# The values of a dilated attention layer: one product of 512 columns per group and four heads, in place of 256 + 256 columns of two groups for two heads

## Chip, cores and metric

One core of one Trainium2 chip runs the kernel in one launch. The metric is the device time of a run in microseconds (us); three runs of the kernel before took 2038.84 to 2041.54, median 2041.24.

## The reference, cut to what matters

Two blocks follow each other: a hybrid attention layer with a mixture of experts, and then a second block with two layers, of which "layer A" is the first. All is float32, 512 tokens of width 1024. Layer A projects the normed tokens to queries, keys and values for three dilation groups of eight heads of width 128, lets each group attend within its own dilated window, and adds the three results with weights from their log-denominators; four further heads read a memory of 256 tokens.

```
DIL_PAIRS = ((128, 1), (512, 4), (2048, 16))          # (window, dilation) of groups 0, 1, 2
qkv = cols.reshape(B, S, 3, N_GROUPS_2, A_HEADS, HEAD_DIM)
q = rms_norm(qkv[:, :, 0], q_gain[:, None, :])
k = rms_norm(qkv[:, :, 1], k_gain[:, None, :])
v = qkv[:, :, 2]                                        # no norm, no rotation
...
for g, (window, dil) in enumerate(DIL_PAIRS):
    o, lse = dilated_window_attention(q[:, :, g], k[:, :, g], v[:, :, g], dil, window // dil)
alpha = jax.nn.softmax(jnp.stack(lses, axis=0), axis=0)
o = jnp.sum(alpha[..., None] * jnp.stack(outs, axis=0), axis=0)
```

## The kernel before, in words

**Products.** A float32 product is made of three matmuls of float32r parts: each operand is split into a high and a low part, and mm3 (L359 to L361) adds high x high, high x low and low x high. The normed, transposed tokens stand in hT, eight pairs of [128 rows of the width, 512 tokens]. A product "natural" takes 128 tokens of hT as the stationary operand (weights of the array, loaded by LDWEIGHTS) and 512 columns of the weight matrix as the moving operand, eight row blocks one after another into one PSUM bank: 24 matmuls, called a pass below; four passes make the 512 tokens.

**Two orders of the tokens.** Tile c holds either the tokens 128 c to 128 c + 127 (run, a plain slice of hT) or the tokens 4 a + c (comb, every fourth element of hT, a slice with a stride of four). Group 0 of the queries, keys and values uses run, groups 1 and 2 use comb. In the text a matmul whose stationary operand is such a slice is called plain or combed.

**Values before.** Per pair of heads, v01_block (L1615) fills one PSUM bank per tile with two products of 256 columns: group 0, plain, in columns 0 to 255, and group 1, combed, in columns 256 to 511. The two halves have different norm factors, so two instructions of 256 columns (L1627) bring them to an SBUF tile of 512. For every second pair, v_block (L1605) makes group 2 for four heads, combed, 512 columns, brought out by one instruction (L1610). The tiles have the tag v, ten places.

**The loop of layer A.** It runs over four pairs of heads (L1762 on). A pair has, in the order of the program: its values (v01_block; in pairs 0 and 2 also v_block of group 2), three qk_block (queries and keys of one group for both heads: a natural product of 512 columns, a norm per head, rotation, four transposes, written to the tag qk of twelve places, all used by a pair), two gate blocks (L1638), and attend_A for each of the two heads. attend_A makes four tiles of scores (L1673, L1676), a softmax on VectorE and ScalarE, transposes (L1681) and the products with the values: groups 1 and 2 of tile c as soon as tile c is there (L1685, L1686), group 0 of all tiles at the end of the head (L1691). So a value tile of groups 1 and 2 comes free within the pair's second head, one of group 0 at its end. After the loop mem_attend handles the memory's heads; its split_kv puts eight tiles into v, its queries eight into qk.

**Order of the work.** The Tile framework's scheduler orders each engine's instructions: by the order of the program, but an instruction may go ahead of earlier ones that wait, as long as its tiles have places. The products of the next pair thus go between the matmuls of a pair's attention. Product sums use the tag acc of two PSUM banks, scores the tag sc of three (at the start of layer A the values use three of sc and one of acc). Weights come in one stream in the order of use: units of 512 KB (two row blocks of 512 columns) are loaded by SyncE's queue into three places wraw, split by ScalarE (L241) and VectorE or, every eighth one, GpSimd (L244), into five places w, each used by 24 matmuls of 512 columns.

Of the kernel before, what the change touches and what calls it, by code (L numbers as in the profile page):

```python
# [11 lines left out]
F32 = mybir.dt.float32  # L12
# [14 lines left out]
NS = 96          # slots of a tile of tokens of one group of experts  # L27


# ---------------------------------------------------------------- host layout  # L30
def _units_k(w, kk):
    """[K, N] -> [K/(128 kk), 128, kk, N]: row blocks, one contiguous run per partition."""
    K, N = w.shape
    return np.ascontiguousarray(w.reshape(K // (128 * kk), kk, 128, N).transpose(0, 2, 1, 3))


def _units_n(w):
    """[K, N] -> [N/128, 128, K/128, 128]: column blocks of 128."""
    K, N = w.shape
    return np.ascontiguousarray(w.reshape(K // 128, 128, N // 128, 128).transpose(2, 1, 0, 3))  # L40


def _cols(v):
    """[128 n] -> [128, n]"""
    return np.ascontiguousarray(v.reshape(-1, 128).T)
# [8 lines left out]
def _nat(t):  # L54
    """[512, n] -> [128, 4, n]"""
    return np.ascontiguousarray(t.reshape(4, 128, -1).transpose(1, 0, 2))


def _constants():
# [22 lines left out]
    # layer A: query 4 a + c in row a of tile c; in group 0 it sees two tiles of 128 keys from BASE[a // 32] on  # L82
# [20 lines left out]
def layout(I):  # L103
# [58 lines left out]
    for hq in range(2):  # L162
        hs0, hs1 = slice(4 * hq, 4 * hq + 2), slice(4 * hq + 2, 4 * hq + 4)
        r = lambda g, hs: v[:, g, hs].reshape(1024, 256)
        vv.append(_units_k(np.concatenate([r(0, hs0), r(1, hs0)], 1), 2))
        vv.append(_units_k(np.concatenate([r(2, hs0), r(2, hs1)], 1), 2))
        vv.append(_units_k(np.concatenate([r(0, hs1), r(1, hs1)], 1), 2))
# [31 lines left out]
# columns of `vecs`  # L199
# [5 lines left out]
class Stream:  # L205
    """Weights in the order of their use: loaded ahead, split into float32r high and low parts."""
# [5 lines left out]
    def lane(self, name, pool, raw, raws, part, parts, pool_every=0, raw_pool=None):  # L212
        """units of this lane are loaded into one of `raws` tiles of tag `raw` and split into one of `parts` pairs"""
        self.lanes[name] = (raw_pool or pool, raw, raws, part, parts, pool_every, pool)
# [32 lines left out]
    def _room(self, first, i, k):  # L247
        """whether there is a place of unit i's tag that none of the units from `first` on takes"""
# [24 lines left out]
    def rows(self, n):  # L273
        """n units of row blocks -> list of (hi, lo) per 128 rows"""
# [7 lines left out]
# steps of the memory's keys and values between the parts of the router, and between the tiles after the experts  # L282
ROUTER = (1, 1, 1, 2, 4, 4, 8)
AFTER = (8, 4, 4, 4, 2, 2)
# products of the next head's q and k, or of the gate, after each level of layer B's scores
FILL = (4, 4, 4, 3, 3, 3, 3)
# steps beside the two attentions of block 1: index scores and products beside the first (its two halves), products
# beside the second
# [3 lines left out]
# when the masks of the best keys are made, in groups of four steps of the first attention  # L292
BEST = {3: 9, 2: 12, 1: 15}
# lanes of the experts' weights: of the first units, then in turns up to units 60, 181 and the end
# [4 lines left out]
def build(tc, A, out, dbg=None):  # L299
# [5 lines left out]
    # ------------------------------------------------------------ pools  # L305
# [23 lines left out]
    # ------------------------------------------------------------ constants  # L329
# [13 lines left out]
    def rsq(pool, ss, n, name="rs", eps=None, ring=""):  # L343
        """(ss / n + eps) ** -0.5 for a [128, m] tile of sums of squares; eps: EPS, or [128, m] or [128, 1]"""
# [12 lines left out]
    def mm3(p, a, b, start, stop):  # L357
        """p += a.T @ b with a, b split into float32r parts; the product of the low parts is below float32."""
# [4 lines left out]
    def split(pool, src, tag, bufs, scale=None):  # L363
        """[128, n] -> float32r high and low parts (of src * scale)."""
# [11 lines left out]
    def row_scale(pool, xs, n=1024):  # L376
        """per-row sums of squares of four natural tiles -> (mean + eps) ** -0.5, [128, len]"""
# [6 lines left out]
    def transposed(xs, gain, pool, tag, bufs, nk=8, banks=(), tps=None, more=None):  # L384
        """natural tiles [128 tok, 128 nk] -> nk pairs (hi, lo) of [128, 128 len(xs)], times a gain per row"""
# [18 lines left out]
    def eps_of(r, name):  # L404
        """EPS / r ** 2: the EPS of a norm of what r has yet to scale"""
# [5 lines left out]
    def norm_tiles(pool, r, combed):  # L411
        """nrm: R the norms r of the rows of four token tiles, RC of the rows 4 a + c, RB along the columns; E, EC: EPS / r ** 2"""
# [15 lines left out]
    def run(c):  # L428
        """token tile c: 128 tokens in a row"""
        return slice(c * 128, c * 128 + 128)  # L430

    def comb(c):
        """token tile c: tokens 4 a + c"""
        return slice(c, None, 4)

    def memory_steps(ws, mT, consume, banks):
        """out[m, 512] = memory @ W for its two tiles of 128, both sums open; consume(c, psum); in steps of one product"""
# [13 lines left out]
    def natural_wide(ws, hT, N, consume, banks):  # L451
        """natural with the four token tiles' sums open"""
# [8 lines left out]
    def natural_steps(ws, hT, N, consume, nunits=4, toks=run, banks=None):  # L461
        """out[tok, N] = h @ W for the four token tiles; consume(c, psum); in steps of one product"""
# [16 lines left out]
    def columns_steps(ws, hT, n, consume, nk=8):  # L479
        """out[128 cols, tok] per column block; consume(j, psum); in steps of one product"""  # L480
# [21 lines left out]
    def pump(steps, n=None):  # L502
        """the next n of the steps, or all that are left"""
# [8 lines left out]
    # ------------------------------------------------------------ streams  # L512
# [21 lines left out]
    for hp in range(4):  # L534
        hq, odd = divmod(hp, 2)
        if odd == 0:
            plan2 += rows_plan(va[3 * hq]) + rows_plan(va[3 * hq + 1])
        else:
            plan2 += rows_plan(va[3 * hq + 2])
# [26 lines left out]
    # ------------------------------------------------------------ shared pieces  # L566
    last = {}

    def softmax_tile(pool, pieces, W, tag):
        """pieces: [(psum ap, mask ap, column)] of negated scores -> normalised weights [128, W]"""  # L570
# [12 lines left out]
    def swap_rope(pool, dst, src, tab, nh, half, eng, tag):  # L583
        """dst, src: [128, nh, 2 half] views; tab: [128, 2, 2 half] = (cos|cos, -sin|sin)"""
# [8 lines left out]
    def outproj(yT, xs, view, after=None):  # L593
        """xs += y @ W, 512 columns at a time with the four token tiles' sums open"""
# [18 lines left out]
    # keys and values of the memory (both layers of the second block)  # L613
    mTd = dr.tile([128, 2048], F32, name="mTd")

    def mem_load(pool):
        """what mem_prep stored, split"""
# [10 lines left out]
    def mem_prep(pool):  # L628
        """the memory's rows normalised, transposed, split for the first layer: 8 pairs of [128 d, 256 m]; stored for
        the second"""  # L630
# [39 lines left out]
    def mem_v(mT, out, banks=(acc, acc)):  # L670
        """values of the memory, in steps of one product: out(c) [128 m, 512] of its tokens 128 c + .."""
        return memory_steps(ws, mT, lambda c, p: S.activation(out(c), p, AF.Copy), banks)

    def mem_k(l, mT, pool, out, banks=(acc, acc)):
        """keys of the memory, in steps of one product and a last one of transposes: out(j) [128 d, 512 (h, m)] of heads 2 j and 2 j + 1"""
# [14 lines left out]
    def head_norm(pool, p, nh, tag, bufs, eps=None, ring=""):  # L690
        """psum [128, 128 nh] -> rows of each head over their root mean square"""
# [10 lines left out]
    # ============================================================ block 1  # L702
# [37 lines left out]
    # c_q, k_r, w_i  # L740
# [40 lines left out]
    def rope_heads(c, p, nh, scale, tag, bufs, dup=False):  # L781
        """natural [128, 64 nh] psum -> scaled, the first 16 of each 64 rotated"""
# [36 lines left out]
    def roped_steps(scale, nat):  # L819
        """the eight heads of 64, natural, in steps of one product"""  # L820
# [9 lines left out]
    # index scores, the 128 best keys of each query  # L830
# [23 lines left out]
    def best(i):  # L854
        """the mask that leaves the 128 best keys of a query"""
# [16 lines left out]
    # MLA, four heads at a time  # L872
# [7 lines left out]
    def attention_steps(prs, lhs, rhs, masks, vt, otag, obufs, res, ahead=2):  # L880
        """pairs of heads of 64: softmax over the keys up to each query tile -> o^T split; in steps of a tile's
        scores, its transposes, or a head's values"""
# [57 lines left out]
    def half_steps(hh):  # L940
        """queries and keys of four heads, in steps of one product"""
# [31 lines left out]
    # DSA  # L973
# [11 lines left out]
    # y = sigmoid(g_a) y_a + sigmoid(g_b) y_b, transposed (the heads' outputs carry the factor 1/2 of the sigmoid)  # L985
    yac, sgb = [], []

    def part_a():
        """in steps of one product"""
# [50 lines left out]
    # ============================================================ router and experts  # L1040
# [86 lines left out]
    # logits of x1 with the gain in the weights; the norm of the row is applied to them  # L1127
# [50 lines left out]
    def first_max(src, n, name):  # L1178
        """src [128, 4, n] -> (max [128, 4], one-hot of its first place [128, 4, n])"""
# [38 lines left out]
    def steps(src, n, name):  # L1218
        """number of whole NS in src"""
# [17 lines left out]
    # weights of the two best experts of the group  # L1237
# [26 lines left out]
    # what a slot has to know of its token: tile + 1, row, 1 / rms (payi); the four weights (payw);  # L1264
    # the last two in three bfloat16 parts
# [20 lines left out]
    def slot_ranks(shift, name):  # L1286
        """[128 tok, NS slots] per token tile: whether the token is of rank shift + slot in its group"""
# [9 lines left out]
    def slot_table(R, pay, n, name):  # L1297
        """[NS slots, 8 groups, n]: what the slot's token of each group wrote"""
# [7 lines left out]
    def slot_rows(t, n, name):  # L1306
        """t [NS, n, 5] -> rows to read and to write (int32 [NS, n]; an empty slot reads row 0 and writes
        row 512 + slot), 1 / rms [NS, n]"""
# [12 lines left out]
    def slot_weights(t, n, name):  # L1321
        """t [NS, n, 12] -> half weights [NS, n, 4]"""
# [31 lines left out]
    def experts(get, X, w, ox):  # L1354
        """the four experts of one group on NS slots: rows of sum_e w_e (silu(x Wg) * (x Wu)) Wd"""
# [60 lines left out]
    # groups with more than NS tokens: at most five further tiles of NS slots  # L1416
# [49 lines left out]
    # x + m, its norm, the input of the second block  # L1466
# [545 lines left out]
```

## Time and profile before

| | us |
|---|---|
| runs | 2041.54, 2038.84, 2041.24; median 2041.24 |
| profiled execution, first to last instruction | 2042.5 |
| PE (TensorE matmul) busy | 1971.9, 97% of the span |
| PEld (weight loads) busy | 1571.2, 77% |
| DVE (VectorE) busy | 1144.4, 56% |
| ACT (ScalarE) busy | 945.9, 46% |
| POOL (GpSimd) busy | 577.0, 28% |

No time outside the span is recorded for the profiled execution; the span itself lies 1.3 us above the median of the runs. Matmuls are pipelined: one's recorded duration overlaps the next one's start, so what a matmul costs in a stream is read from the distance between starts, and idle time of PE from waits. A few matmul records are missing, and a row that says x2 holds two matmuls. Layer A lies between about 898 and 1600 us of the span.

### The profile page before, as it was taken

Reading aid. Unit: us, or ns where it says so; the run is one execution under the profiler, and the core shown is the slowest. Engines: PE = TensorE matmul, PEld = TensorE weight load, DVE = VectorE, ACT = ScalarE, POOL = GpSimd, SP = SyncE. Lnnn points to the kernel's source line nnn. Section 1 sums busy time; section 2 is a strip of 40 time slices with the busy share of each in tenths; the row PEclk is TensorE's granted clock in tenths of the full one; section 3 lists DMA queues with packets and bytes.
Section 4 is the critical chain, followed back from the end, with each engine's and each line's share of the span. In section 5 each row is a group of like instructions: output and inputs, shape, how many; then the busy total and the mean of one; then the engine's idle time right before and its main releaser. Section 6 shows DMA issues by size and latency. Waiting matters only on the chain.

```text
span 2042.5 us, 27315 instructions
## 1 busy us (share of the span) xinstructions
PE 1971.9 (97%) x10138; PEld 1571.2 (77%) x10138; DVE 1144.4 (56%) x1999; ACT 945.9 (46%) x1975; POOL 577.0 (28%) x518
## 2 busy tenths in 40 slices
PE   8999999999899898799999999999999999999999
PEld 8757766787566565589988989888988877777887
DVE  5378744376989986754332341342347344666672
ACT  5454444344667665653443443443456233333460
POOL 2201200011677664631521410530520001222210
PEclk9999999999999998999999999999999999999999
DMA  5211222178788887743211222221223333221231
GB/s 169 78 52 42 62 62 62 52 243 292 262 295 290 328 307 284 248 168 137 83 62 42 83 63 74 84 70 42 83 63 124 103 114 93 63 63 56 70 104 62
DMA packets 77711, 257.08 MB, mean 126 GB/s; under 512 B 10241, under 2 KB 12033, under 8 KB 77569
## 3 DMA queue, kind: packets, MB, share of 16 engines
q1 hardware_dynamic: 74912, 246.33, 36.1%
q0 software_dynamic: 1792, 6.29, 0.9%
q10 hardware_dynamic: 864, 2.62, 0.3%
q8 instruction: 82, 1.34, 0.3%
q14 instruction: 61, 0.49, 0.1%
HBM read 241.58 MB, written 13.63 MB: 125 GB/s over the span
## 4 chain that ended last, share of the span: by engine, by line
PE 54%; DVE 1%; ACT 1%; POOL 0%; issue 0%; DMA 0%; ACTq 0%; DVEq 0%; POOLq 0%
PE acc L359 13%; PE acc L360 13%; PE acc L361 13%; PE sc L359 2%; PE sc L361 2%; PE sc L360 2%; PE sc L1882 1%; PE sc L1673 1%; PE tp L1599 1%; PE sc L1676 1%; PE tp L1681 1%; PE oT L1691 1%; PE oT L1930 1%; ACT whi L241 0%; DVE wlo L244 0%; PE oT L1685 0%
## 5 line engine op out<-in xcount | busy, mean ns | idle before, releaser
L244 DVE TENSOR_TENSOR wlo<-wraw,whi 128x1024 fp32r<-128x1024 f32 (+4 forms) x255 | 335.3, 1321 | 227.9 <-ACT whi L241 226.4
L241 ACT ACTIVATE whi<-wraw 128x1024 fp32r<-128x1024 f32 (+4 forms) x294 | 296.4, 1011 | 296.1 <-PE acc L360 113.7
L359 PE MATMUL acc<-whi,hh 128*128 128x512 f32 (+3 forms) x1040 | 411.0, 397 | 5.2 <-ACT hjk L695 2.6
L360 PE MATMUL acc<-wlo,hh 128*128 128x512 f32 (+3 forms) x1040 | 403.8, 389 | 0.0
L361 PE MATMUL acc<-whi,hl 128*128 128x512 f32 (+3 forms) x1040 | 400.6, 387 | 0.0
L359 PEld LDWEIGHTS acc<-whi,hh 128*128 128x128 f32 x1040 | 249.4, 240 | 32.2 <-issue 5.6
L360 PEld LDWEIGHTS acc<-wlo,hh 128*128 128x128 f32 x1040 | 250.2, 241 | 20.5 <-issue 1.5
L361 PEld LDWEIGHTS acc<-whi,hl 128*128 128x128 f32 x1040 | 249.3, 240 | 21.2 <-issue 0.8
L244 POOL TENSOR_TENSOR wlo<-wraw,whi 128x1024 fp32r<-128x1024 f32 (+3 forms) x39 | 96.8, 2485 | 490.3 <-ACT whi L241 490.2
L354 POOL TENSOR_TENSOR rs<-rsa,mhalf 128x4 f32<-128x4 f32 (+1 forms) x80 | 81.7, 1021 | 377.1 <-DVE rsa L351 301.8
L359 PE MATMUL acc<-hh,whi 128*128 128x512 f32 x448 | 186.3, 416 | 0.0
L361 PE MATMUL acc<-hh,wlo 128*128 128x512 f32 x448 | 177.5, 396 | 0.0
L360 PE MATMUL acc<-hl,whi 128*128 128x512 f32 x448 | 176.8, 395 | 0.0
L244 POOL TENSOR_TENSOR mlo<-xn,mhi 128x1024 fp32r<-128x1024 f32 x47 | 131.7, 2808 | 70.1 <-ACT mhi L241 70.0
L244 DVE TENSOR_TENSOR mlo<-mraw,mhi 128x1024 fp32r<-128x1024 f32 x49 | 101.0, 2065 | 20.1 <-ACT mhi L241 20.0
L695 ACT ACTIVATE hjk<-acc 128x128 bf16<-128x128 f32 x232 | 64.3, 277 | 100.2 <-PE acc L361 75.5
L359 PEld LDWEIGHTS acc<-hh,whi 128*128 128x128 f32 x448 | 84.5, 189 | 25.6 <-issue 8.5
L361 PEld LDWEIGHTS acc<-hh,wlo 128*128 128x128 f32 x448 | 84.2, 188 | 19.0
L360 PEld LDWEIGHTS acc<-hl,whi 128*128 128x128 f32 x448 | 84.6, 189 | 15.8 <-issue 0.9
L360 PE MATMUL acc<-mlo,xgh 128*96 128x512 f32 x180 | 73.9, 411 | 14.6 <-DVE mlo L244 9.5
L241 ACT ACTIVATE mhi<-mraw 128x1024 fp32r<-128x1024 f32 x63 | 66.4, 1055 | 43.8 <-PE acc L361 16.8
L361 PE MATMUL sc<-whi,hl 128*128 128x512 f32 (+4 forms) x200 | 75.1, 380 | 3.1 <-DVE hl L370 2.4
(556 smaller groups left out, 3750.6 us busy)
## 6 DMA issues: line engine op xcount, KB each, us to landing
mraw<-in_w_moe SPq DMA_DIRECT2D x60, 512.0 KB, 4.9
xn<-in_w_moe SPq DMA_DIRECT2D x60, 512.0 KB, 4.7
wraw<-in_w_moe SPq DMA_DIRECT2D x54, 512.0 KB, 5.0
wraw<-in_w_qka SPq DMA_DIRECT2D x48, 512.0 KB, 4.1
wraw<-in_w_va SPq DMA_DIRECT2D x24, 512.0 KB, 4.0
wraw<-in_w_qfb SPq DMA_DIRECT2D x16, 512.0 KB, 3.5
mT<-in_w_moe SPq DMA_DIRECT2D x14, 512.0 KB, 4.7
wraw<-in_w_vb SPq DMA_DIRECT2D x12, 512.0 KB, 3.5
```

What stands on the lines that cost most here:

```text
L241: nc.scalar.activation(hi, raw, AF.Copy)
L244: eng.tensor_tensor(lo, raw, hi.bitcast(F32), OP.subtract)
L354: G.tensor_tensor(r[:, :m], t[:, :m], mhalf[:, :m], OP.pow)
L359: T.matmul(p, a[0], b[0], start=start, stop=False)
L360: T.matmul(p, a[0], b[1], start=False, stop=False)
L361: T.matmul(p, a[1], b[0], start=False, stop=stop)
L695: S.activation(jk, p[:, h * 128:h * 128 + 128], AF.Square, accum_out=st[:, h:h + 1])
L1599: T.transpose(tp[:, c * 128:c * 128 + 128], nat[c][:, j * 128:j * 128 + 128], ident)
L1673: T.matmul(p[32 * j:32 * j + 32, :256], q0[:, 128 * j + c:128 * j + 128:4], k0[:, 128 * BASE[j]:128 * BASE[j] + 256], start=True, stop=True)
L1676: T.matmul(p[:, 128 + g * 128:256 + g * 128], qk[g][s][:, cs], qk[g][2 + s][:, cs], start=True, stop=True)
L1681: T.transpose(tp[:, j * 128:j * 128 + 128], pt[:, j * 128:j * 128 + 128], ident)
L1691: T.matmul(o3[:, :, a0:a1], v01[b + x][:, s * 128:s * 128 + 128], PT0[:, x, :].rearrange("p (c a) -> p c a", c=4)[:, :, a0:a1], start=Fals ...
```

## The change

The weight matrix of the values is laid out per group and four heads. v01_block goes; v_block makes all three groups, each as one product of 512 columns for four heads, before pair 0 and before pair 2; pairs 1 and 3 have no value products. The tag v has 13 places in place of 10, of which 12 are held from one set of values to the next. To make room, the four last chunks of the layer's output (tag yc, four places) take places of the tag qk. attend_A reads the columns of its head among four.

```
 layout():
     for hq in range(2):
-        hs0, hs1 = slice(4 * hq, 4 * hq + 2), slice(4 * hq + 2, 4 * hq + 4)
-        r = lambda g, hs: v[:, g, hs].reshape(1024, 256)
-        vv.append(_units_k(np.concatenate([r(0, hs0), r(1, hs0)], 1), 2))
-        vv.append(_units_k(np.concatenate([r(2, hs0), r(2, hs1)], 1), 2))
-        vv.append(_units_k(np.concatenate([r(0, hs1), r(1, hs1)], 1), 2))
+        for g in range(3):
+            vv.append(_units_k(v[:, g, 4 * hq:4 * hq + 4].reshape(1024, 512), 2))
 the stream of weights:
-        if odd == 0:
-            plan2 += rows_plan(va[3 * hq]) + rows_plan(va[3 * hq + 1])
-        else:
-            plan2 += rows_plan(va[3 * hq + 2])
+        for g in range(3):
+            if odd == 0:
+                plan2 += rows_plan(va[3 * hq + g])
-    def v_block(pool, tag, bufs, toks=run):
+    def v_block(pool, tag, bufs, toks=run, banks=None):
...
-        natural(ws, hT, 512, use, toks=toks)
+        natural(ws, hT, 512, use, toks=toks, banks=banks)
-    def v01_block(banks=(acc,) * 4):
-        w = ws.rows(4)
-        res = []
-        for c in range(4):
-            p = banks[c]()
-            for n, toks in enumerate((run, comb)):
-                q = slice(256 * n, 256 * n + 256)
-                for k in range(8):
-                    mm3(p[:, q], tuple(z[:, toks(c)] for z in hT[k]), tuple(z[:, q] for z in w[k]), k == 0, k == 7)
-            t = pa.tile([128, 512], F32, name="v", tag="v", bufs=10)
-            for q, r in ((slice(0, 256), "R"), (slice(256, 512), "RC")):
-                nc.any.tensor_scalar(t[:, q], p[:, q], nrm[r][:, c:c + 1], None, OP.mult)
-            res.append(t)
-        return res
-    ych, ytag = [], ("yc", 4)
+    ych, ytag = [], ("qk", 12)
 attend_A(h, qk, v):
+        vs = slice((h % 4) * 128, (h % 4) * 128 + 128)
...
-            T.matmul(oT[:, cs], v01[c][:, 256 + s * 128:384 + s * 128], PT[:, :128], start=c == 0, stop=False)
-            T.matmul(oT[:, cs], v2[c][:, v2off + s * 128:v2off + s * 128 + 128], PT[:, 128:],
-                     start=False, stop=False)
+            T.matmul(oT[:, cs], v[1][c][:, vs], PT[:, :128], start=c == 0, stop=False)
+            T.matmul(oT[:, cs], v[2][c][:, vs], PT[:, 128:], start=False, stop=False)
...
-                T.matmul(o3[:, :, a0:a1], v01[b + x][:, s * 128:s * 128 + 128],
+                T.matmul(o3[:, :, a0:a1], v[0][b + x][:, vs],
 the loop:
-        if not odd:
-            vA[0] = v01_block((scp, scp, scp, acc) if hp == 0 else (acc,) * 4)
-            vA[1] = v_block(pa, "v", 10, comb)
-        else:
-            vA[0] = v01_block()
+        if hp % 2 == 0:
+            vA = [v_block(pa, "v", 13, comb if g else run, (scp, scp, scp, acc) if hp + g == 0 else None)
+                  for g in range(3)]
...
-    mem_attend(pa, 0, split_kv(pa, kvA, 10), y, 12, 3)
+    mem_attend(pa, 0, split_kv(pa, kvA, 13), y, 12, 3)
```

## Rows read from the trace of the kernel before

**Rows 1.** The page: the span, and TensorE's busy time, share and instructions.

```profile
span 2042.5 us, 27315 instructions
...
PE 1971.9 (97%) x10138; PEld 1571.2 (77%) x10138; DVE 1144.4 (56%) x1999; ACT 945.9 (46%) x1975; POOL 577.0 (28%) x518
```

**Rows 2.** Stretches of layer A: length, busy us (instructions) per engine, clock, DMA.

```profile
935.00:1047.00 112.00, 112.00 (x506) 102.61 (x506) 45.02 (x91) 51.49 (x140) 47.20 (x67) 1.00 0.32 107
1237.00:1359.00 122.00, 122.00 (x564) 112.77 (x564) 39.38 (x46) 51.89 (x137) 44.82 (x63) 1.00 0.28 91
1503.00:1549.00 46.00, 46.00 (x279) 37.06 (x278) 24.78 (x55) 25.15 (x73) 4.04 (x4) 1.00 0.21 68
```

**Rows 3.** Waits of PE, 898 to 1560 us: total us, times, longest.

```profile
PE acc L359 <- ACT hjk L695: 2.6, 2, 1.3
PE acc L359 <- DVE nat L698: 1.0, 2, 0.7
PE sc L361 <- DVE hl L373: 0.7, 1, 0.7
```

**Rows 4.** Groups of one shape, L359: matmuls of 256 columns on token slices.

```profile
L359 PE MATMUL acc<-whi,hh 128*128 128x256 f32 x208 | 71.9, 346 | 0.0
L359 PE MATMUL sc<-whi,hh 128*128 128x256 f32 x48 | 16.2, 339 | 0.0
```

**Rows 5.** Timeline of PE (start, duration): plain 256, then combed 256.

```profile
902.26 0.28 PE L359 MATMUL sc<-whi,hh 128*128 128x256 f32 x1
...
904.52 0.28 PE L360 MATMUL sc<-wlo,hh 128*128 128x256 f32 x1
...
929.55 0.40 PE L359 MATMUL acc<-whi,hh 128*128 128x256 f32 x1
...
934.99 0.40 PE L361 MATMUL acc<-whi,hl 128*128 128x256 f32 x1
```

**Rows 6.** Timeline of the weight loads in the same two stretches.

```profile
902.50 0.19 PEld L359 LDWEIGHTS sc<-whi,hh 128*128 128x128 f32 x1
...
930.12 0.33 PEld L359 LDWEIGHTS acc<-whi,hh 128*128 128x128 f32 x1
```

**Rows 7.** Timeline of PE: combed 512 (group 2's values), then plain 512.

```profile
939.86 0.40 PE L359 MATMUL acc<-whi,hh 128*128 128x512 f32 x1
...
944.66 0.40 PE L361 MATMUL acc<-whi,hl 128*128 128x512 f32 x1
...
965.33 0.40 PE L359 MATMUL acc<-whi,hh 128*128 128x512 f32 x1
...
974.90 0.40 PE L361 MATMUL acc<-whi,hl 128*128 128x512 f32 x1
```

**Rows 8.** Instructions that write v, 935 to 1560 us: ns min/median/max, times, forms.

```profile
L1627 ACT ACTIVATE v<-acc,R x12: 474/475/476, 1057.0 to 1413.5; 128x256 f32<-128x256 f32 x12
...
L1610 ACT ACTIVATE v<-acc,RC x8: 688/688/692, 945.1 to 1270.0; 128x512 f32<-128x512 f32 x8
```

**Rows 9.** Stretches, products into acc alone: PE, PEld, DVE, ACT busy us.

```profile
1047.00:1092.00 45.00, 26.64 (x138) 24.54 (x137) 1.18 (x2) 1.42 (x3) 1.00 0.05 16
1192.00:1227.00 35.00, 19.63 (x104) 18.22 (x104) 0.95 (x2) 1.41 (x3) 1.00 0.05 16
1503.00:1549.00 46.00, 27.60 (x112) 20.21 (x110) 3.37 (x5) 5.86 (x32) 1.00 0.21 68
```

**Rows 10.** Timeline of PE: pair 1's second head reads its first value tiles.

```profile
1227.49 0.38 PE L1685 MATMUL oT<-PT,v 128*128 128x128 f32 x2
```

**Rows 11.** The weights' raw tiles, 898 to 1560 us: landing time of their DMAs.

```profile
DMA to landing us min/median/max: 3.3/4.1/7.3
```

**Rows 12.** Timeline of DVE: last gate of pairs 1, 2 and 3 (idle before, releaser).

```profile
1191.78 0.69 DVE L1638 TENSOR_TENSOR gt<-acc,RB 128x512 f32<-128x512 f32 x1 [3.11 <-PE acc L361]
...
1358.37 0.69 DVE L1638 TENSOR_TENSOR gt<-acc,RB 128x512 f32<-128x512 f32 x1 [1.94 <-PE acc L361]
...
1502.92 0.69 DVE L1638 TENSOR_TENSOR gt<-acc,RB 128x512 f32<-128x512 f32 x1 [2.88 <-PE acc L361]
```

More of the change, by code (lines that the diff above doesn't have):

```diff
@@ L1662, in ychunk, with attend_A @@
         return pool.tile([128, 512], F32, name="yc", tag=ytag[0], bufs=ytag[1])
-    def attend_A(h, qk, v01, v2, v2off):
+    def attend_A(h, qk, v):
         s = h % 2
+        vs = slice((h % 4) * 128, (h % 4) * 128 + 128)
         oT = otp()
@@ L1760, in build @@
     y = []
-    vA = {}
     for hp in range(4):
-        hq, odd = divmod(hp, 2)
-        if not odd:
-            vA[0] = v01_block((scp, scp, scp, acc) if hp == 0 else (acc,) * 4)
-            vA[1] = v_block(pa, "v", 10, comb)
-        else:
-            vA[0] = v01_block()
+        if hp % 2 == 0:
+            vA = [v_block(pa, "v", 13, comb if g else run, (scp, scp, scp, acc) if hp + g == 0 else None)
+                  for g in range(3)]
         qk = [qk_block(g) for g in range(3)]
@@ L1774, in build @@
         for s in range(2):
-            oT = attend_A(2 * hp + s, qk, vA[0], vA[1], 256 * odd)
+            oT = attend_A(2 * hp + s, qk, vA)
             y.append(gated(pa, oT, g2[s], combed=True))
-    mem_attend(pa, 0, split_kv(pa, kvA, 10), y, 12, 3)
+    mem_attend(pa, 0, split_kv(pa, kvA, 13), y, 12, 3)
     for j in range(12):
```

## The prediction, made before the changed kernel ran

> **What bounds the kernel now.** I read the page first: PE is busy for 97% of the span, every other engine for under 60% of it except the weight loads, which run beside matmuls [rows 1]. [...] Third, the waits of PE over the whole of the stage: 4.3 us in 662, in five pieces [rows 3]. So a matmul taken out of layer A shortens the run, unless its absence opens a wait. What a matmul costs must then come from the timeline, as the distance between starts.
>
> **The products.** There are 208 + 48 = 256 matmuls of 256 columns on each of the three lines of mm3, 768 in all [rows 4]. By the code that is 4 pairs x 4 tiles x 8 row blocks x 3 = 384 plain ones and as many combed ones, and their mean durations of 346 and 339 ns mix two kinds. Apart they are:
> - plain, 256 columns: 20 starts from 902.26 to 904.52, 19 distances, 0.1189 us [rows 5];
> - combed, 256 columns: 24 starts from 929.55 to 934.99, 23 distances, 0.2365 us [rows 5];
> - combed, 512 columns (group 2's values, unchanged by the edit): 21 starts from 939.86 to 944.66, 0.2400 us [rows 7];
> - plain, 512 columns: 42 starts from 965.33 to 974.90, 0.2334 us [rows 7].
>
> A combed matmul thus costs the same for 256 columns as for 512. Its weight load shows why: 0.33 us against 0.19 for a plain slice of the same 128 x 128 [rows 6]. The load runs ahead beside the matmul before it; beside 512 columns the longer one is hidden, beside 256 it sets the pace. Removed: 384 x 0.1189 = 45.7 us and 384 x 0.2365 = 90.8 us. Added: 192 x 0.2334 = 44.8 us (group 0) and 192 x 0.2400 = 46.1 us (group 1). Sum: 90.9 - 136.5 = -45.6 us, nearly all of it from group 1. All four prices are in the trace; with 0.2365 for the combed 512 it is -46.3.
>
> [...]
>
> **Bringing the values out.** Before: 32 instructions of 256 columns at 0.475 us and 8 of 512 at 0.688 [rows 8], 20.7 us; after: 24 of 512, 16.5 us. They run on ACT and DVE beside PE, which these engines follow with half of their time free [rows 2]: 0.
>
> **Weights.** The 24 units of values stay the same bytes. Four units of pair 1 (and of pair 3) move ahead of 12 units of queries and keys and two of gates: their loads in SP's queue, their splits in ACT's, and DVE's or POOL's. The rings and the count that gives every eighth split to POOL are as before, so nothing is put behind a longer wait; only the demand in the values rises, from a unit per 6 x (0.1189 + 0.2365) x 4 = 8.5 us of PE to one per 24 x 0.2334 = 5.6. The query and key blocks already run at that pace without a wait in pairs 0 and 2 [rows 2], with loads that land in 4.1 us (7.3 at most) [rows 11]. I take 0. If that cover failed, the seam between blocks would look like the waits of the page's stage, about 1 us each [rows 3].
>
> **What fills the attention.** This is the step with a price that the trace does not show. Between the last gate of a pair and the end of its attention PE has work of the next pair: 26.6 of 45 us are products into acc, all of them v01_block's [rows 9]. What stands there afterwards differs by pair.
> - Pairs 0 and 2 are followed by qk_block: five places of nat and two banks of acc allow 7 passes of 5.6 us, 39 us, where 26.6 are used. They add a norm per pass on ACT, DVE and POOL. The nearest row is pair 3, filled by the memory's queries with the same norm: 27.6 us of products in 46, PE never idle, ACT at 25 of 46 [rows 2, 9]. I take 0.
> - Pair 1 is followed by values. Before, 10 places less 8 held leave 2, and with acc 4 passes of 8.5 us. Afterwards 13 less 12 leave 1, so 3 passes of 5.6 us, 16.8 us, until a value tile is free; the first is read for the last time when the pair's second head does its first product with values, at 1227.49 [rows 10]. Up to 1227 this attention took in 19.6 us of products [rows 9]. PE is short of 19.6 - 16.8 = 2.8 us. Ends: 0, if the attention, less interrupted, frees the tile earlier; 8.4, if one more pass stays out. I take +2.8.
> - Pair 3 keeps its fill. split_kv needs eight places of v: four tiles each of groups 1 and 2 come free during the last head, where before there were two places and four tiles. 0.
>
> **Waits that may go.** The 3.6 us of waits at L359 for a norm (ACT hjk, DVE nat) [rows 3] are not in the products of pairs 0 and 2 [rows 2], so they belong to the pairs whose qk_block follows a v01_block. That seam is gone; the new one, inside the attention, may have its own. Ends -3.6 and +3.6; I take half of what goes, -1.8. The 0.7 us at the start (hl, L373) [rows 3] come while the token chunks of hT arrive; there a chunk feeds 12 plain matmuls, 1.4 us of work, afterwards 2.8. I count nothing.
>
> **Room for the output.** In the memory's attention qk holds eight query tiles and four output chunks, 12 of 12. Each query tile is free once its head's scores are done. Taken as 0; if a chunk had to wait, a gate pass of 5.6 us lies beside it on PE, and that is the high end.
>
> **Sum.** -45.6 + 2.8 - 1.8 = -44.6. The profiled execution's span is 2042.5 [rows 1], so 1997.9; it lies 1.3 above the median of the runs, 2041.24, so 1996.6, about 1997. Ends of the likeliest case: -46.3 - 3.6 gives 1991, with the start's 0.7 about 1990; -45.6 + 5.6 + 3.6 gives 2005.
>
> **The rivals.**
> - *The columns are the price* (no gain): a combed 256 would cost 0.1189 like a plain one, and 0.2365 would be an effect of that stretch alone. Then 768 x 0.1189 = 91.3 goes and 384 x 0.2334 = 89.6 comes: 2039.5. Against it: both kinds lie in the same block within 30 us at the same clock, and the load's duration differs with the slice [rows 5, 6]. [...]
> - *Part of the fill is lost*: the norms of the query and key passes load ACT and DVE while these make the softmax, so the passes between pairs 0 and 1 and between 2 and 3 come out slowly and acc blocks. Half of 26.6 lost twice is 26.6 us: 2023; an eighth to a half gives 2003 to 2023. For it: ACT is at 25 of 46 in pair 3 [rows 2]. Against it: PE has no idle time there.
> - *Slower*: the scheduler finds no fill in any of the four attentions, because the held value tiles and the full qk ring keep the next pair's work out, and each runs bare. At half of these products [rows 9] that is 4 x 13.3 = 53 us, 2050; it decides from 44.6 / 4 = 11.2 us per pair. Against it: nat and acc alone hold 39 us.
> - *More*: waits hidden inside PE's busy time at the 256-column seams go too, 7 us or more beyond the sum: under 1990.
>
> **How the numbers follow.** Likeliest 0.74, no gain 0.03, part of the fill lost 0.15, slower 0.04, more 0.04. The likeliest and its own range: 1997, 1990 to 2005. The range for 8 in 10 runs from 1989 to 2012, which takes in the smaller half of the lost fill and leaves out no gain, slower, most of "more" and the larger half: 0.17. What a measurement can tell from no change is 0.2%, 4 us. Faster: 0.74 + 0.15 + 0.04 = 0.93; within: 0.03; slower: 0.04.
>
> **What would show it.** The groups of one shape should have no matmul of 256 columns on L359 to L361 with whi and token slices in layer A, and 384 more of 512; combed ones at 0.24 us between starts and 0.31 to 0.33 us per load. From one pair's last gate to the next one's it was 166.6 us for pair 2 and 144.6 for pair 3 [rows 12]; pair 3 should take 144.6 - 34.1 - 1 = about 110, pair 2 166.6 - 34.1 + 45.4 + 2.8 = about 181. PE should wait in the attention of pair 1 for some 3 us, for a value tile's place. The prediction is wrong if combed 512 lies well above 0.24, if PE waits more than 10 us in the attentions, or if pairs 1 and 3 do not become shorter by over 30 us each.

## The result, and the profile after

The changed kernel takes 1990.24 us (median of four runs, 1988.43 to 1995.10); the kernel before, beside it, 2041.39 (four runs, 2038.84 to 2045.86). The ratio is 0.9753, 95% interval 0.9734 to 0.9771: 50.4 us less by the ratio (0.0247 x 2041.4), 51.1 by the medians. A gain of 44.6 us was forecast, so the forecast lies 5.8 us short of the gain by the ratio and 6.5 by the medians. The time is inside the range, but at the lower edge of the likeliest case, which ran from 1990 to 2005 around 1997.

The page of the changed kernel, the answer to [rows 1]: span, then busy time, share and instructions of each engine.

```profile
span 1987.3 us, 26527 instructions
...
PE 1920.4 (97%) x9754; PEld 1513.9 (76%) x9754; DVE 1139.7 (57%) x2003; ACT 939.6 (47%) x1955; POOL 578.6 (29%) x518
```

384 matmuls fewer, 51.5 us less of busy PE, and the same share of 97%. The two spans differ by 55.2 us, which is more than the medians do. The starts of the first value product and of the first transpose behind layer A's output show where. Before (start, duration, engine, line, operation):

```profile
898.52 0.28 PE L359 MATMUL sc<-whi,hh 128*128 128x256 f32 x1
...
1650.63 0.27 PE L390 MATMUL sc<-c_ident,x 128*128 128x128 f32 x1
```

After:

```profile
895.13 0.39 PE L356 MATMUL sc<-whi,hh 128*128 128x512 f32 x1
...
1595.62 0.27 PE L387 MATMUL sc<-c_ident,x 128*128 128x128 f32 x1
```

Layer A, taken here up to the end of its output's product, went from 752.1 to 700.5 us: 51.6 of the 55.2. The 3.4 ahead of it lie in code that the change does not touch. The same start falls between 893.7 and 898.9 in the runs told of below, and at 898.15 in a second trace of the changed kernel (e8), so they are the spread of single executions and no part of the effect.

The groups of one shape after, answer to [rows 4] (count, busy us and mean ns, idle time ahead):

```profile
L356 PE MATMUL acc<-whi,hh 128*128 128x512 f32 x904 | 373.2, 414 | 1.6 <-ACT hh L369 0.6 <-ACT v L1606 0.5 <-ACT nat L780 0.4
...
L356 PE MATMUL sc<-whi,hh 128*128 128x512 f32 x120 | 47.5, 397 | 0.0
```

The two groups of 256 columns are gone from this list, and these two hold 1024 matmuls where before they held 896: 128 more on each of three lines, the 384 of the forecast. Note that the mean duration, 414 and 397 ns, says nothing of what one costs. The distance between starts does; PE's timeline of group 1's values, combed, 34 starts, and of group 0's, plain, 30 starts:

```profile
904.19 0.40 PE L356 MATMUL sc<-whi,hh 128*128 128x512 f32 x1
...
910.94 0.39 PE L358 MATMUL sc<-whi,hl 128*128 128x512 f32 x1
...
922.16 0.40 PE L356 MATMUL acc<-whi,hh 128*128 128x512 f32 x1
...
930.08 0.40 PE L356 MATMUL acc<-whi,hh 128*128 128x512 f32 x1
```

(930.08 - 922.16) / 33 = 0.2400 and (910.94 - 904.19) / 29 = 0.2328 us, where [rows 7] gave 0.2400 and 0.2334. The weight load of a combed slice is recorded with 0.31 us, where 0.31 to 0.33 was forecast:

```profile
925.04 0.31 PEld L357 LDWEIGHTS acc<-wlo,hh 128*128 128x128 f32 x1
```

The value tiles come out in instructions of 512 columns, 21 on ACT at 0.69 us, as group 2's in [rows 8], and 3 on DVE at 0.75.

Now the waits of PE. Between 894 and 1560 us the view has its header and not one row; before it had three, 4.3 us [rows 3]. The stretch from just ahead of the first value product to 1548 says the same (length, busy us of PE, PEld, DVE, ACT and POOL, clock, DMA):

```profile
894.00:1548.00 654.00, 654.00 (x3288) 578.46 (x3287) 278.02 (x499) 306.14 (x805) 185.94 (x263) 1.00 0.26 85
```

PE is busy in all of it at a granted clock of 1.00. So the expected wait for a value tile's place in pair 1's attention is not there. The last gates of pairs 0 to 3 on DVE:

```profile
1053.87 0.69 DVE L1618 TENSOR_TENSOR gt<-acc,RB 128x512 f32<-128x512 f32 x1 [2.52 <-PE acc L358]
...
1162.66 0.69 DVE L1618 TENSOR_TENSOR gt<-acc,RB 128x512 f32<-128x512 f32 x1 [2.90 <-PE acc L358]
...
1339.31 0.69 DVE L1618 TENSOR_TENSOR gt<-acc,RB 128x512 f32<-128x512 f32 x1 [3.27 <-PE acc L358]
...
1448.07 0.69 DVE L1618 TENSOR_TENSOR gt<-acc,RB 128x512 f32<-128x512 f32 x1 [2.89 <-PE acc L358]
```

Against [rows 12]: pair 2 takes 176.65 us (166.59 before, 181 forecast) and pair 3 108.76 (144.55 before, 110 forecast). Pair 1 takes 108.79, where it took 144.78 from the last gate of pair 0 in the kernel before:

```profile
1047.00 0.69 DVE L1638 TENSOR_TENSOR gt<-acc,RB 128x512 f32<-128x512 f32 x1 [1.94 <-PE acc L361]
```

So pairs 1 and 3 became shorter by 36 us each.

### The profile page after: what moved, and what is told of

The parts are those of the page before. It is cut to its first block, busy times and chain, and to the rows that moved or that the text cites. A ratio compares the mean times of both kernels' runs of the same rounds, so it can differ in the third digit from the quotient of the medians.

```text
span 1987.3 us, 26527 instructions
## 1 busy us (share of the span) xinstructions
PE 1920.4 (97%) x9754; PEld 1513.9 (76%) x9754; DVE 1139.7 (57%) x2003; ACT 939.6 (47%) x1955; POOL 578.6 (29%) x518
## 4 chain that ended last, share of the span: by engine, by line
PE 54%; DVE 1%; ACT 1%; POOL 0%; issue 0%; ACTq 0%; POOLq 0%
PE acc L356 13%; PE acc L357 13%; PE acc L358 13%; PE sc L356 2%; PE sc L357 2%; PE sc L358 2%; PE sc L1858 1%; PE sc L1654 1%; PE tp L1595 1%; PE sc L1657 1%; PE tp L1662 1%; PE oT L1671 1%; PE oT L1906 1%; PE oT L1666 0%; ACT whi L238 0%; DVE wlo L241 0%
## 5 line engine op out<-in xcount | busy, mean ns | idle before, releaser
L356 PE MATMUL acc<-whi,hh 128*128 128x512 f32 (+2 forms) x936 | 384.3, 412 | 1.6 <-ACT hh L369 0.6
L358 PE MATMUL acc<-whi,hl 128*128 128x512 f32 (+2 forms) x936 | 371.9, 400 | 0.0
L357 PE MATMUL acc<-wlo,hh 128*128 128x512 f32 (+2 forms) x936 | 371.8, 398 | 0.0
L356 PEld LDWEIGHTS acc<-whi,hh 128*128 128x128 f32 x936 | 223.5, 239 | 30.8 <-issue 4.9
L357 PEld LDWEIGHTS acc<-wlo,hh 128*128 128x128 f32 x936 | 224.1, 240 | 21.8 <-issue 1.5
L358 PEld LDWEIGHTS acc<-whi,hl 128*128 128x128 f32 x936 | 222.7, 239 | 22.5 <-issue 0.8
L356 PE MATMUL acc<-mhi,xgh 128*96 128x512 f32 x180 | 72.4, 407 | 6.0 <-DVE th L1363 6.0
```

The lines of the kernel that those rows point to most:

```text
L356: T.matmul(p, a[0], b[0], start=start, stop=False)
L357: T.matmul(p, a[0], b[1], start=False, stop=False)
L358: T.matmul(p, a[1], b[0], start=False, stop=stop)
```

## The experiments

The theory: a combed matmul costs what its weight load allows, whether it has 256 columns or 512, so nearly all of the gain is group 1's, and the rest is the waits at the old seams. The rival: the number of matmuls is what costs, or the order and the room in the rings brings the gain. All times are medians; ratios are to the kernel before, run beside each kernel on the same chip.

**The changed kernel again (e8).** No edit: it is what the other kernels are compared with, ratio against ratio.

> The changed kernel itself beside the others on this chip, as their common base. Expected 0.975 of before, about 1991.

1989.72 us; 0.9739 (0.9726 to 0.9753).

**The old kernel without the comb in the values (e1).** Same matmuls, same order, and group 1's values read a plain slice.

```
-            for n, toks in enumerate((run, comb)):
+            for n, toks in enumerate((run, run)):
```

> The kernel before, with group 1's values computed from the plain token slices in place of the combed ones: still 256 + 256 columns, same number of matmuls, same rings and order (group 1's values then belong to the wrong tokens). Theory (the combed weight load sets the pace of a 256-column matmul): 384 matmuls go from 0.2365 to 0.1189 us, -45 us against before, about 1996. Rival (the columns are the price, 0.2365 belonged to that one stretch; the gain of the change came from order and waits): no change, 2041. If the theory holds, PE's waits of 3.6 us at the seam to the query and key block may stay.

1998.24; 0.9779 (0.9765 to 0.9792), 44.5 us less than before. Not one matmul fewer, and nearly the whole gain is there. In its trace, the timeline of group 1's values (PE, 23 starts, and one weight load among them):

```profile
918.98 0.28 PE L360 MATMUL acc<-wlo,hh 128*128 128x256 f32 x1
...
920.05 0.19 PEld L361 LDWEIGHTS acc<-whi,hl 128*128 128x128 f32 x1
...
921.59 0.28 PE L361 MATMUL acc<-whi,hl 128*128 128x256 f32 x1
```

The load is 0.19 us and the distance 0.1186, where combed ones had 0.33 and 0.2365 [rows 5, 6]. What it leaves are the waits of PE in layer A:

```profile
PE acc L359 <- ACT hjk L695: 3.5, 3, 1.3
PE sc L361 <- DVE hl L373: 0.7, 1, 0.7
PE acc L359 <- DVE nat L698: 0.4, 1, 0.4
```

4.6 us in all, against [rows 3]: these do not come from the comb.

**The new kernel with group 1 in halves (e2).** Each tile's sum as two products of 256 columns again; all else is the new kernel.

```
+            for q in (slice(0, 256), slice(256, 512)):
+                for k in range(8):
+                    mm3(p[:, q], tuple(z[:, toks(c)] for z in hT[k]), tuple(z[:, q] for z in w[k]), k == 0, k == 7)
...
-            vA = [v_block(pa, "v", 13, comb if g else run, (scp, scp, scp, acc) if hp + g == 0 else None)
+            vA = [v_block(pa, "v", 13, comb if g else run, (scp, scp, scp, acc) if hp + g == 0 else None, g)
```

> The changed kernel with its order and rings, but group 1's values (combed) made as two products of 256 columns per tile. Theory: 384 x 0.2365 in place of 192 x 0.2400, +44.7 us against the changed kernel, about 2035. Rival (columns are the price): +0.8, 1991.

2034.91; 0.9959 (0.9945 to 0.9972). Against e8 that is 0.0220 x 2042.7 = 44.9 us given back, by 192 matmuls more. The halves run at the price of whole ones, here (935.10 - 930.20) / 21 = 0.2333 us. A load is recorded with 0.33 us, longer than that, so one begins before the last has ended:

```profile
930.06 0.33 PEld L357 LDWEIGHTS acc<-wlo,hh 128*128 128x128 f32 x1
...
930.20 0.40 PE L357 MATMUL acc<-wlo,hh 128*128 128x256 f32 x1
...
935.10 0.40 PE L357 MATMUL acc<-wlo,hh 128*128 128x256 f32 x1
```

**The new kernel with group 0 in halves (e3).** The same edit for g == 0: again 192 matmuls more, plain ones.

> The changed kernel, but group 0's values (plain) made as two products of 256 columns per tile. Theory: 384 x 0.1189 in place of 192 x 0.2334, +0.8 us, about 1991. Rival (the number of matmuls is the price, each instruction having a floor near 0.23 us): +45, 2035.

1994.20; 0.9762 (0.9748 to 0.9775), 0.0023 above e8 or 4.7 us. With intervals of 2.7 us on both, that is between some 1 and 8.5 us, more than the 0.8 forecast but not the 45 that a price per matmul asks; against the first measurement of the changed kernel (0.9753) it is 1.8. Its trace has layer A at 703.5 us, 3.0 above the changed kernel, and the pace is half a whole one's (40 starts, 0.1187):

```profile
905.82 0.28 PE L356 MATMUL sc<-whi,hh 128*128 128x256 f32 x1
...
907.01 0.19 PEld L358 LDWEIGHTS sc<-whi,hl 128*128 128x128 f32 x1
...
910.45 0.28 PE L356 MATMUL sc<-whi,hh 128*128 128x256 f32 x1
```

The same weight load (0.19 us), half the columns, half the price (0.1187 us against 0.2328 and 0.2334). The wait at the start of layer A is back in it, 0.7 us for hl; with the 0.8 that makes 1.5 of the 3.0.

**The new kernel without the comb in the values (e4).**

```
-            vA = [v_block(pa, "v", 13, comb if g else run, (scp, scp, scp, acc) if hp + g == 0 else None)
+            vA = [v_block(pa, "v", 13, run, (scp, scp, scp, acc) if hp + g == 0 else None)
```

> The changed kernel with all three groups' values computed from plain token slices (groups 1 and 2 then belong to the wrong tokens), 512 columns. Theory (512 columns hide the combed load): 384 x (0.2400 - 0.2334) = -2.5 us, about 1988. Rival (the longer load still costs what it cost beside 256 columns, 0.118 us each): -45, 1945.

1987.95; 0.9734 (0.9721 to 0.9748): the comb, worth 45 us at 256 columns, is worth nothing that these runs resolve at 512. In the trace layer A is 2.8 us shorter, as 384 x (0.2400 - 0.2334) = 2.5 says (25 starts, 0.232):

```profile
930.12 0.19 PEld L356 LDWEIGHTS acc<-whi,hh 128*128 128x128 f32 x1
...
930.34 0.39 PE L356 MATMUL acc<-whi,hh 128*128 128x512 f32 x1
...
935.91 0.40 PE L356 MATMUL acc<-whi,hh 128*128 128x512 f32 x1
```

**The new order alone (e5).** The new kernel with the halves of e2 in groups 0 and 1 (g in (0, 1)): the matmuls of the old kernel in the order and the rings of the new one.

> The changed kernel's order and rings with groups 0 and 1 both made as two products of 256 columns: the same 384 plain and 384 combed matmuls of 256 columns as in the kernel before, but per group and before pairs 0 and 2. What is left against before is order and seams. Theory (the waits of 4.3 us sat at the seam from values to queries and keys of pairs 1 and 3, which is gone): about -5 us against before, and PE without a wait of over 0.3 us in the pairs. Rival (the waits come with the 256-column products): no change against before, waits still there.

2036.58 (11 runs); 0.9974 (0.9965 to 0.9983), so 5.3 us less than before, 3.5 to 7.1. Its waits of PE, from before the first value product on:

```profile
PE sc L395 <- DVE hl L370: 1.0, 1, 1.0
PE sc L358 <- DVE hl L370: 0.7, 1, 0.7
```

The first row lies ahead of layer A. Of the pairs' waits none is left.

**The new rings alone (e7).** The old kernel with 13 places of v and the output chunks in qk.

```
-            t = pa.tile([128, 512], F32, name="v", tag="v", bufs=10)
+            t = pa.tile([128, 512], F32, name="v", tag="v", bufs=13)
...
-    ych, ytag = [], ("yc", 4)
+    ych, ytag = [], ("qk", 12)
...
-            vA[1] = v_block(pa, "v", 10, comb)
+            vA[1] = v_block(pa, "v", 13, comb)
...
-    mem_attend(pa, 0, split_kv(pa, kvA, 10), y, 12, 3)
+    mem_attend(pa, 0, split_kv(pa, kvA, 13), y, 12, 3)
```

> The kernel before with only the rings of the change: 13 places of v, the four last output chunks in qk. Theory (rings cost and bring nothing): within 2 us of before. Rival (the places, not the products, gave part of the gain): -5 us against before, with the 3.6 us of waits gone.

2042.45 (11 runs); 0.9996 (0.9987 to 1.0005). The room alone gives nothing, and the waits stay:

```profile
PE acc L359 <- ACT hjk L695: 3.1, 3, 1.3
PE sc L398 <- DVE hl L373: 1.0, 1, 1.0
PE sc L361 <- DVE hl L373: 0.7, 1, 0.7
PE acc L359 <- DVE nat L698: 0.4, 1, 0.4
```

L398's row, like L395's in e5, lies ahead of layer A. With e1 and e5 this places the others: they stay while the values of every pair come just ahead of its queries, and go when the loop's order is the new one. As the prediction inferred, they lie in pairs 1 and 3: in the kernel before, PE is idle for 1.95 us between 1092 and 1192 and for 1.68 between 1403 and 1503, and for none in the products of pairs 0 and 2 [rows 2].

**Twelve places for the values (e6).** The held tiles then take all of v, and no tile of pair 2's values has a place until pair 1's second head gives one free.

```
-            vA = [v_block(pa, "v", 13, comb if g else run, (scp, scp, scp, acc) if hp + g == 0 else None)
+            vA = [v_block(pa, "v", 12, comb if g else run, (scp, scp, scp, acc) if hp + g == 0 else None)
...
-    mem_attend(pa, 0, split_kv(pa, kvA, 13), y, 12, 3)
+    mem_attend(pa, 0, split_kv(pa, kvA, 12), y, 12, 3)
```

> The changed kernel with 12 places of v in place of 13: no place free when pair 1's attention begins, so two passes of values (11.2 us, in the two acc banks) can stand beside it. Theory (an attention that gets less fill runs denser and ends earlier; that is why 13 places cost nothing): no change, at most +1 us. Rival (the fill sets PE's idle time there, as the prediction had it): one pass less, +5.6 us, as waits of PE in pair 1's attention.

1990.18; 0.9743 (0.9730 to 0.9756), the time of e8. The fill did shrink, and its cost did not come. Pair 1's attention in this kernel, from the last gate to the last output, on DVE's timeline:

```profile
1164.74 0.69 DVE L1618 TENSOR_TENSOR gt<-acc,RB 128x512 f32<-128x512 f32 x1 [2.87 <-PE acc L358]
...
1199.98 0.69 DVE L1681 SCALAR_TENSOR_TENSOR yx<-oT,gt 128x512 f32<-128x512 f32 x1 [7.20 <-PE oT L1671]
```

The stretch between them, busy us per engine, first of all tiles:

```profile
1165.00:1200.00 35.00, 34.85 (x229) 27.98 (x228) 14.18 (x39) 14.51 (x36) 0.00 (x0) 1.00 0.05 16
```

and then of the products into acc alone:

```profile
1165.00:1200.00 35.00, 16.32 (x67) 12.14 (x66) 1.19 (x2) 0.69 (x1) 1.00 0.05 16
```

The same attention's last output in the changed kernel (its last gate, 1162.66, stands above):

```profile
1203.65 0.69 DVE L1681 SCALAR_TENSOR_TENSOR yx<-oT,gt 128x512 f32<-128x512 f32 x1 [0.56 <-PE oT L1671]
```

Its stretch, all tiles:

```profile
1163.00:1204.00 41.00, 41.00 (x255) 32.93 (x254) 18.67 (x43) 18.35 (x39) 0.00 (x0) 1.00 0.10 29
```

and acc alone:

```profile
1163.00:1204.00 41.00, 23.13 (x93) 16.68 (x92) 1.10 (x2) 1.38 (x2) 1.00 0.10 29
```

Take the acc products off the length: 41.0 - 23.1 = 17.9 us here, 35.0 - 16.3 = 18.7 in e6, and 45 - 26.6 = 18.4 in the kernel before, by pair 0's attention [rows 9]. In the two new kernels the same number of matmuls is left without those into acc, 255 - 93 = 229 - 67 = 162. An attention is some 18 us of PE's own work, and, with 16 to 27 us of others' products in it, lasts as much longer as they take. With less fill it ends sooner, and PE stands still for 0.15 us. What an attention does with less than 16 us of fill no run shows.

**Other strides in the old kernel (e9, e10).** Every second and every third token in place of every fourth, in the old kernel's group 1.

```
-            for n, toks in enumerate((run, comb)):
+            for n, toks in enumerate((run, lambda c: slice(c, c + 255, 2))):
```

```
-            for n, toks in enumerate((run, comb)):
+            for n, toks in enumerate((run, lambda c: slice(c, c + 382, 3))):
```

> The kernel before with the token slices of group 1's values at a stride of two elements in place of four (the values then belong to the wrong tokens); counts, columns and order as before. Open: whether any stride lengthens the weight load, or only one as long as four. If any stride does: as before, 2042, load 0.33 us, 0.2365 us per matmul of 256 columns. If the price grows with the bytes between two elements: load between 0.19 and 0.33, a time between 1998 and 2042. If eight bytes are free: load 0.19, like the all-plain run, about 1998. [...]

> The same with a stride of three elements (12 bytes). If the price grows with the bytes: load about three quarters of the way or two thirds between 0.19 and 0.33, a time between the runs with strides of two and four. [...] If any stride of over two has the full price: 2042.

Stride 2: 2000.13; 0.9797 (0.9777 to 0.9817), as fast as a plain slice (e1) within the intervals. Stride 3: 2017.90; 0.9884 (0.9864 to 0.9904), between the plain slice and the comb, about half way. The timeline with stride 2 and a load in it:

```profile
919.79 0.28 PE L361 MATMUL acc<-whi,hl 128*128 128x256 f32 x1
...
920.14 0.20 PEld L359 LDWEIGHTS acc<-whi,hh 128*128 128x128 f32 x1
...
922.31 0.28 PE L361 MATMUL acc<-whi,hl 128*128 128x256 f32 x1
```

With stride 3:

```profile
920.79 0.34 PE L361 MATMUL acc<-whi,hl 128*128 128x256 f32 x1
...
923.18 0.27 PEld L360 LDWEIGHTS acc<-wlo,hh 128*128 128x128 f32 x1
...
924.57 0.34 PE L361 MATMUL acc<-whi,hl 128*128 128x256 f32 x1
```

22 starts each: 0.120 and 0.180 us. Stride 2 came out as the last of e9's three cases, load and time: 0.20 us where that case has 0.19, 2000 where it has about 1998. Stride 3 has a load of 0.27 us, a little over half of the way from 0.19 to 0.33 and less than the two thirds or three quarters of a price by bytes.

**Layer A by itself.** The time from the first value product to the first transpose behind layer A's output, read in each trace as above, leaves out what happens elsewhere in an execution:

| kernel | layer A, us |
|---|---|
| before | 752.1 |
| before, new rings (e7) | 751.9 |
| new order, both halved (e5) | 746.7 |
| group 1 halved (e2) | 744.5 |
| before, stride 3 (e10) | 730.0 |
| before, stride 2 (e9) | 709.1 |
| before, plain (e1) | 708.5 |
| group 0 halved (e3) | 703.5 |
| 12 places (e6) | 700.7 |
| changed | 700.5 |
| changed again (e8) | 700.4 |
| changed, plain (e4) | 697.7 |

Each is one execution, but the two of the changed kernel lie 0.1 us apart, where the medians of the whole run are uncertain by 2 to 4. By these the new order without any product saved brings 5.4 us (752.1 to 746.7) and the whole products 46.2 (746.7 to 700.5), 51.6 together.

## Why the prediction was right, and where it was off

**The products, -45.6: right.** From e5 to the changed kernel layer A loses 46.2 us, which are these products and the 0.7 of the start below. e2 and e3 give the halves back one at a time: 44.9 us for group 1 (192 x (2 x 0.2365 - 0.2400) = 44.7 by the rows) and, less certain, 4.7 for group 0, where the rows have 0.8 and the start 0.7. Three of the four prices came out as read. The combed 256 has two values, and the prediction's stretch shows the higher one: of seven unbroken stretches of over 20 starts in the trace of before two have 0.237 and five 0.233, such as this one (23 starts, 0.2332):

```profile
1096.56 0.39 PE L360 MATMUL acc<-wlo,hh 128*128 128x256 f32 x1
...
1101.69 0.40 PE L361 MATMUL acc<-whi,hl 128*128 128x256 f32 x1
```

With 0.2333 throughout the term would be -44.4; what decides between the two is open. e1 shows the cause from the other side: without the comb the old kernel has 44.5 of it, with all its 256-column matmuls. The rival "columns are the price" is out by the result, and by e2 on its own. In a stream of loads and matmuls the traces show 0.119 us for 256 columns behind a load of 0.19, and 0.2333 behind one of 0.33.

**Bringing out, weights, room in qk, 0 each: in agreement.** PE has no wait up to the end of layer A's output that could belong to one of them; the rings alone (e7) change nothing.

**The fill of pair 1's attention, +2.8: this step failed.** The prediction said that "PE is short of 19.6 - 16.8 = 2.8 us". It took the attention's length from the trace of before as given, and asked what would fill it. But that length is mostly fill: 19.6 of the 35 us up to 1227 [rows 9]. The count of three passes was right: in the changed kernel 17.6 us of acc products, 71 recorded matmuls of the 72 of three passes, stand in the 32 us up to the second head's first product with values (at 1195.06), two under the 19.6 of before. But PE is busy throughout; the row is of acc alone:

```profile
1163.00:1195.00 32.00, 17.64 (x71) 12.61 (x69) 0.35 (x1) 0.69 (x1) 1.00 0.06 18
```

The attention takes 41.0 us from gate to last output (1162.66 to 1203.65) where it took 44.6 (1191.78 [rows 12] to 1236.36, the last output before):

```profile
1236.36 0.69 DVE L1701 SCALAR_TENSOR_TENSOR yx<-oT,gt 128x512 f32<-128x512 f32 x1 [11.68 <-PE oT L1691]
```

e6 cuts the fill once more and gets 35.2, with the time of the whole kernel unchanged. A product left out of this attention was done behind it at the same price: layer A takes 700.7 us in e6 and 700.5 in the changed kernel. The stated end of 0 was the right value, with its reason: the tile's last reader comes 32.4 us after the gate, where it came after 35.7.

**Waits that go, -1.8: half of what went.** All 3.6 us of [rows 3] at L359 went and nothing came in their place, the end of the range that was not taken. The new order without any product saved (e5) is worth 5.3 us (3.5 to 7.1), and 5.4 in layer A, so it carries these 3.6 and, by layer A, 1.8 more that no wait shows; where they lie is open.

**The start's 0.7, taken as nothing: gone too.** The prediction counted the work per token chunk rightly (2.8 us in place of 1.4) and did not draw the conclusion: it went with 512-column products at the start (in the changed kernel, e2, e4, e6) and is there with 256-column ones (e1, e3, e5, e7).

Together 2.8 + 1.8 + 0.7 = 5.3 us, and by these terms the sum is -45.6 - 3.6 - 0.7 = -49.9 against -50.4, which is uncertain by 3.8. In layer A it is -51.6, 1.7 more, about what the order carries beyond the waits.

**The other rivals.** "Part of the fill is lost" and "slower" are out: no idle time of PE in any attention. "More" needed hidden waits of 7 us beyond the sum; the gain comes to its edge, but with a fill that was not lost and waits that the view had shown, and only the order's 1.8 are hidden. From gate to gate pair 3 came out as forecast; pair 2 took 4.3 us less than forecast, 2.8 of which are the fill that was not lost.

**What stays open.** Why the waits at the old seam were there is argued only: a pass of queries ends when both acc banks wait for a norm. The runs show that the order decides it, not the comb and not the rings. Where the other 1.5 us of e3's 3.0 in layer A lie is open as well.

## What to carry to other kernels

Read a matmul's price as the distance between starts, per shape and per layout of the stationary operand, and beside it the duration of its weight load. In these runs a stationary slice with a stride of three or four elements set a floor per matmul, 0.180 and 0.233 to 0.237 us, which 256 columns paid in full (0.119 with a plain slice) and 512, run at stride four, hid (0.2400 against 0.2334). Where it must stay strided, give each load 512 columns; where the columns must stay few, a slice of stride 1 or 2 does the same (0.119 and 0.120 us for 256). When fill is moved out of a stage, take the stage's own work, not its recorded length, as what is to be filled; how far down that holds is to be tried.

## What the runs showed of the hardware

The load's duration and the price of a 256-column matmul follow the stride of the stationary slice (float32r, 128 x 128, a mean granted clock of 0.99 in each profiled run), though not from the first step on:

| stride | load, us | between starts, 256 columns, us | kernel | median, us |
|---|---|---|---|---|
| 1 | 0.19 | 0.119 | e1 | 1998.24 |
| 2 | 0.20 | 0.120 | e9 | 2000.13 |
| 3 | 0.27 | 0.180 | e10 | 2017.90 |
| 4 | 0.33 | 0.233 to 0.237 | before | 2042.77, 2043.18 |

Stride 2 costs nothing that the medians resolve (0.6 us in layer A); from there each step adds 0.06 to 0.07 us to the load and 0.05 to 0.06 to the distance. From stride 3 on the distance is the load less 0.09 to 0.10; as nothing but the stationary slice differs, it is the load that sets the pace. At stride 4 it asks for 0.233 to 0.237, hardly more than the 0.2334 that 512 plain columns take: hence nearly the same price for both combed widths, and hence two combed products of 256 columns at almost twice the price of one of 512. Other element sizes were not run.

Half way between the values of stride 1 and stride 4 lie 0.26 us for the load and 0.18 for the distance; stride 3 has 0.27 and 0.180. Why the step from stride 1 to 2 costs next to nothing and the two after it do not, no run shows. The 128 columns of a load alone do not give its duration: it is 0.27 and 0.33 us at strides 3 and 4 against 0.19 at stride 1.
